# Seven PSUM banks for the first projection, one mixer chunk and one memory weight split earlier, and one sum of squares moved, in a one-core decoder-trunk kernel

## The chip, the cores and the metric

The kernel runs on one core of a Trainium2 chip. The metric is the device time of one execution in microseconds. Three runs of the kernel before took 1888.49, 1888.15 and 1880.31 us; their median is 1888.15.

## What is computed

One layer of a decoder trunk, for a prompt of 1024 tokens and for 8 samples of 4 tokens that look back on 4096 cached positions in pages. The reference, cut to what matters here:

```python
h = rms_norm(x, g_mix)
u, v, cq, ckv, kpe = split_in(h @ w_in)                 # first projection
a_out = gelu(u) * mixed(layer_norm(gelu(v)), w_s, b_s)  # gMLP, chunks of 128
ckv_n = rms_norm(ckv)
q = mla_queries(cq); k, vv = mla_keys_values(ckv_n, kpe)
b_out = attend(q, k, vv)          # prompt: causal; samples: pages of the cache
x = x + concat(rms_norm(a_out), rms_norm(b_out)) @ w_o  # mixer, out projection
mk, mv = mem_kv(rms_norm(mem))                          # 256 memory tokens
x = x + mem_attend(rms_norm(x), mk, mv)
x = x + conv_ffn(rms_norm(x))
```

All matrix products keep single precision by splitting each operand into a high and a low part and adding three products (`mm3`, L185: high with high, low with high, high with low). A split is a rounding cast on ACT (L191, or L195 with a gain) and a subtraction on DVE (L192, L198).

## The kernel before

The 1056 tokens (1024 of the prompt, 32 of the samples) form nine tiles (`TILES`, eight of 128 and one of 32) and three chunks (`CH`: 384, 384, 288). Work follows in stages, each with its own pools of PSUM banks: `phase1` (the first projection), `phase2a` (the prompt's attention), `phase2b` (the samples' attention), `mem_kv`, `mixed`, `out_proj`, `mem_attention`, and the feed-forward part.

*First projection.* `phase1` has a pool `ps1` with five banks "mm" for products and three "st" for small ones. In the loop over two halves (`hf`) it makes v for nine tiles (`proj`, 24 matmuls each), then u for nine tiles, then the gate products. An evicting Gelu on ACT (L435) scales by `rs_tok`, the root of the token's sum of squares, which `squares` (L332 on ACT) and `rsqrt` (a chain of small DVE steps, L222 to L236) make for tiles 0, 1 and 2, 3 to 5 and 6 to 8. `gate_matrices` makes the small constants: `wsc` (POOL, L392) and two products into "st" (L394, L396), which DVE reads at L398.

*Prompt attention.* `phase2a` projects queries (q), keys (k) and values (v) from the latents (`cqh`, `ckh`) for groups of two tiles. A group is a pair of lists of steps: the first makes q and k, the second v. The q and k of groups 0 to 3 run ahead of the transposes; their v runs after the first transposes. From there a table of steps written out by hand sets the order on PE, ACT, DVE and POOL. At its end `mix_steps` normalises the prompt's outputs `b_all`: squares on ACT (L1501), roots on DVE, scaling on ACT (L1506), four transposes on PE (L1511), a copy on DVE (L1512) and a store to `mix_dram`. The roots sit in a ring of two buffers ("mixr"). At the same time `pth`, the transposed probabilities, are copied on ACT (L928) for the value products (L938), and POOL works on sums of down-projection weights (L778 to L781).

*Samples' attention.* `phase2b` runs 128 numbered steps, again in a written order; `at(n, pos, f)` puts a function into step n. In the last steps four raw loads (two of the memory tokens, two of the weights `w_mk`) are issued. Behind it `mem_kv` makes keys and values of the memory: per head a weight is split (`stream`), and the keys are scaled by a product with diagonal matrices ("diag", L1470, L1471). The latents of the last sample are folded (L1380) and copied on ACT (`olT`, L1381), and `end` (L1171) projects them with `wuv`.

*Mixer.* `mixed` loads the normalised rows of `mix_dram` through three raw buffers, two of eight rows at a time, and splits them into `mx0`, `mx1`, `mx2`, one pair per chunk; SP issues its loads in written order: w_o 0, chunk 0, w_o 1, chunk 1, chunk 2. `mixed_sample` adds the samples' part (`n`, L1551 to L1556). `out_proj` multiplies by eight weight tiles and sums squares of the result per chunk in `acc` (POOL, L1603). At its end the three sums over the partitions (L270) and three roots `r3` follow; then `mem_attention` starts with the query products (`query`), 24 matmuls for each head and chunk.

Where no order is written, the recording layer places instructions on each engine by its own ranking.

Of the kernel before, what the change touches and what calls it, by code (L numbers as in the profile page):

```python
# [154 lines left out]
class Net:  # L155
# [132 lines left out]
    def phase1(self):  # L288
        nc, tc, I, O = self.nc, self.tc, self.I, self.O
        p = self.open("p1")  # L290
        pp = self.open("ps1", space=PSUM)
# [87 lines left out]
        def gate_matrices():  # L379
# [13 lines left out]
            st = self.t(pp, [P, 512], F32, "st", 3)  # L393
# [17 lines left out]
        for hf in range(2):  # L411
# [185 lines left out]
    def phase2a(self):  # L597
# [72 lines left out]
        for g in groups[:4]:  # L670
            extra[0] += self.proj_group(p, pp, 0, *g, st[0], c)[1]
# [20 lines left out]
        with tc.manual_schedule(engines={E.PE, E.Activation, E.DVE, E.Pool}):  # L692
# [13 lines left out]
            def mix(G, ring):  # L706
# [3 lines left out]
                yield from self.mix_steps(pm, pp, 1, 2 * G, 2 * G + 2, lambda i: self.b_all[G][:, i % 2], hl, None, ("tp", 4))  # L710
# [345 lines left out]
    def phase2b(self):  # L1056
        nc, tc, I = self.nc, self.tc, self.I
        pa = self.pa3 = self.open("p3a", side="right")
        pt, p = self.open("p3t"), self.open("p3")
# [25 lines left out]
        for n in range(5):  # L1085
            at(2 * n + 2, 0, lambda: next(mix, 0))
        for b in range(NB):
# [22 lines left out]
        def steps(n0, n1):  # L1110
            for n in range(n0, n1):
# [7 lines left out]
                if n > last - 8 and n % 2 == 0 and len(raws) < 4:  # L1119
                    raw = self.t(p, [P, 4, 288], F32, "ck", 15).rearrange("p k n -> p (k n)")[:, : 8 * P]  # L1120
                    src = (I["memT"][:, :4], I["memT"][:, 4:], I["w_mk"][0], I["w_mk"][1])[len(raws)]
# [27 lines left out]
        with tc.manual_schedule(engines={E.SP}):  # L1149
# [5 lines left out]
            mem = self.mem_kv(raws)  # L1155
# [242 lines left out]
    def mem_kv(self, raws):  # L1398
# [10 lines left out]
        mr = [r.rearrange("p (k n) -> p k n", k=4) for r in raws[:2]]  # L1409
# [3 lines left out]
        for h in range(4):  # L1413
            w = self.stream(I["w_mk"][h], 8, raw=raws[2 + h].rearrange("p (k n) -> p k n", k=8) if h < 2 else None)
# [51 lines left out]
        for h in range(4):  # L1466
            bc = self.t(pp, [P, 512], F32, "b", 2)[:, :256]
            for i in range(2):
                dg = self.t(p, [P, P], F32, "diag", 4)
# [20 lines left out]
    def mix_steps(self, p, pp, z, i0, i1, src, hl, nt, tt):  # L1490
# [14 lines left out]
        for i, n in enumerate(ns):  # L1505
            nc.scalar.activation(n, src(i0 + i)[:tn], AF.Copy, scale=r[:, i : i + 1])  # L1506
        yield
        for i, n in enumerate(ns):
# [10 lines left out]
    def mixed(self):  # L1519
# [3 lines left out]
        px = self.open("mx")  # L1523
        pm = self.pm = self.open("pm")
        mxs = [None] * 3
        for c in (0, 2, 1):
            o, n = CH[c]
            if c == 1:
                self.acc = [self.t(pm, [P, 384], F32, f"acc{e}") for e in range(3)]
                self.t(pm, [P, 384], F32, "sqx", 3)  # L1530
            mxs[c] = [self.t(px if c == 0 else pm, [P, 8, n], FR, f"mx{c}{x}") for x in "hl"]
# [28 lines left out]
    def out_proj(self, pp, p, mxs, ws, xh, xl, r3, end):  # L1560
# [45 lines left out]
    def mem_attention(self, xh, xl, r3):  # L1606
        nc, tc, I, O = self.nc, self.tc, self.I, self.O
        pq = self.open("pq")
        pp = self.open("psa", space=PSUM)
        ps_, p = self.open("pas"), self.open("pa")  # L1610
# [105 lines left out]
        def sample_values():  # L1716
# [3 lines left out]
            pT = self.t(ps_, [P, 2, P], F32, "pT")  # L1720
# [16 lines left out]
            sd = self.t(ps_, [P, P], F32, "sd")  # L1737
# [6 lines left out]
        for h in range(4):  # L1744
# [474 lines left out]
def build(tc, I, O, stop=99, tap=None):  # L2219
# [29 lines left out]
    r3 = N.t(xp, [P, 9], F32, "r3")  # L2249
    po = N.open("po")  # L2250
# [45 lines left out]
```

## Time and profile before

| | |
|---|---|
| median of three runs | 1888.15 us |
| profiled execution | 1886.88 us, span 1885.2 us |
| PE, DVE, ACT, POOL busy | 97%, 73%, 49%, 38% |
| mean granted PE clock | 0.986 |

A row by time gives start, duration, engine, line, operation, output and inputs, shape, and in brackets the idle time of the engine just before it and what released it. A row of the windows view gives busy times and the granted clock of a stretch: 1.00 is full speed. The rows of PE that matter stand in the prediction.

### The profile page before, as it was taken

To read this page: it belongs to the slowest core of one execution; us is meant where nothing else is said; L and a number is where in the kernel's file an instruction comes from. 1 tells how busy PE (TensorE), PEld (TensorE's weight loads), DVE (VectorE), ACT (ScalarE), POOL (GpSimd) and SP (SyncE) were. 2 spreads that over 40 slices of the span, in tenths; PEclk is the share of its full clock that TensorE was granted. 3 is DMA by queue.
4 is the path that set the end of the run, shared out by engine and by line. 5 is a ranking of instruction groups with operands and counts; after the bars stand their busy time and mean duration, and the time that the engine had idled before them with its cause. 6 is when DMAs were issued, how large, how long until landed. Compare 5 with 4: busy or idle time off the path is not lost.

```text
span 1885.2 us, 39848 instructions
## 1 busy us (share of the span) xinstructions
PE 1824.5 (97%) x14402; PEld 1756.9 (93%) x14402; DVE 1382.3 (73%) x2883; ACT 929.7 (49%) x1965; POOL 713.4 (38%) x826
## 2 busy tenths in 40 slices
PE   6999899999999999999999999999999999999999
PEld 6999798889999999998799988999999999999999
DVE  6865868666777667877644576788898888888664
ACT  6435676666555555555543355633332333344442
POOL 1221406643545454544213100157777677500000
PEclk9999899999999999999999999999999999999999
DMA  8102203667776566564554335422222222395242
GB/s 289 65 10 69 80 1 130 254 223 194 209 205 179 168 187 171 169 182 145 169 166 134 135 132 164 130 79 70 87 73 93 78 69 80 99 362 164 79 153 76
DMA packets 139783, 260.18 MB, mean 138 GB/s; under 512 B 20545, under 2 KB 82850, under 8 KB 136514
## 3 DMA queue, kind: packets, MB, share of 16 engines
q1 hardware_dynamic: 138722, 256.58, 43.3%
q8 instruction: 114, 1.87, 0.4%
q10 hardware_dynamic: 864, 1.05, 0.2%
q14 instruction: 83, 0.68, 0.1%
HBM read 212.27 MB, written 45.30 MB: 137 GB/s over the span
## 4 chain that ended last, share of the span: by engine, by line
PE 75%; DVE 8%; DMA 5%; issue 5%; ACT 3%; SPq 2%; POOL 1%; DVEq 0%; POOLq 0%; ACTq 0%
PE s L185 13%; PE d L185 12%; PE mm L185 8%; PE b L185 7%; PE F L185 7%; PE X L185 6%; PE E L185 6%; PE A L185 3%; PE y L185 3%; PE o L938 2%; DMA cT<-cT 2%; PE tp L926 1%; SPq L1212 1%; PE tp L185 1%; PE o L1359 1%
## 5 line engine op out<-in xcount | busy, mean ns | idle before, releaser
L185 PE MATMUL s<-w2h,ch 128*128 128x288 f32 (+1 forms) x1024 | 303.7, 297 | 0.0
L185 PE MATMUL s<-w2h,cl 128*128 128x288 f32 (+1 forms) x1024 | 296.0, 289 | 4.7 <-POOL cl L1244 4.7
L185 PE MATMUL s<-w2l,ch 128*128 128x288 f32 (+1 forms) x1024 | 294.6, 288 | 0.0
L185 PEld LDWEIGHTS s<-w2h,ch 128*128 128x128 f32 x1024 | 192.6, 188 | 8.3 <-issue 3.7
L185 PEld LDWEIGHTS s<-w2h,cl 128*128 128x128 f32 x1024 | 192.4, 188 | 6.9 <-POOL cl L1244 6.7
L185 PEld LDWEIGHTS s<-w2l,ch 128*128 128x128 f32 x1024 | 192.8, 188 | 0.0
L1287 DVE TENSOR_REDUCE ss<-sq 128x16 f32<-128x1024 f32 x128 | 155.6, 1215 | 44.6 <-ACT sq L1284 43.9
L1244 POOL TENSOR_TENSOR cl<-cT,ch 128x512 fp32r<-128x512 f32 x64 | 83.3, 1302 | 122.0 <-ACT ch L1240 90.1
L1284 ACT ACTIVATE sq<-s 128x512 f32<-128x512 f32 x128 | 76.6, 598 | 93.8 <-PE s L185 93.8
L1281 ACT ACTIVATE sq<-s 128x512 f32<-128x512 f32 x128 | 76.9, 600 | 78.3 <-PE s L185 78.3
L191 ACT CAST a<-brb 128x528 fp32r<-128x528 f32 x77 | 48.8, 634 | 112.9 <-PE d L185 107.4
L185 PE MATMUL mm<-whi,xh 128*128 128x256 f32 (+3 forms) x288 | 84.3, 294 | 14.8 <-ACT xh L195 10.0
L192 DVE TENSOR_TENSOR a<-brb,a 128x528 fp32r<-128x528 f32 x77 | 54.1, 705 | 58.5 <-ACT a L191 58.4
L185 PE MATMUL d<-a,w 128*128 128x264 f32 x768 | 95.4, 284 | 0.4 <-DVE G L2075 0.4
L185 PEld LDWEIGHTS d<-a,w 128*128 128x128 f32 x768 | 94.3, 188 | 0.6 <-issue 0.6
L185 PE MATMUL mm<-wlo,xh 128*128 128x256 f32 (+3 forms) x288 | 83.8, 294 | 0.0
L185 PE MATMUL mm<-whi,xl 128*128 128x256 f32 (+3 forms) x288 | 83.3, 293 | 0.0
L938 PEld LDWEIGHTS o<-v,pth 128*128 128x128 f32 x576 | 75.7, 197 | 5.1 <-ACT pth L928 3.4
L1946 POOL TENSOR_TENSOR lo<-s,hi 128x1024 fp32r<-128x1024 f32 x20 | 62.9, 3144 | 45.7 <-ACT hi L1945 45.7
L938 PE MATMUL o<-v,pth 128*128 128x64 f32 x576 | 76.1, 274 | 2.1 <-ACT pth L928 2.0
L2001 ACT COPY a<-A 128x264 f32<-128x264 f32 x43 | 16.1, 375 | 118.7 <-PE A L185 113.9
L1240 ACT CAST ch<-cT 128x512 fp32r<-128x512 f32 x128 | 73.5, 628 | 1.3 <-DMA cT<-cT 1.3
(709 smaller groups left out, 6471.1 us busy)
## 6 DMA issues: line engine op xcount, KB each, us to landing
cT<-cT SPq DMA_DIRECT2D x256, 160.0 KB, 2.7
ck<-ck SPq DMA_DIRECT2D x256, 144.0 KB, 3.5
raw<-w_up SPq DMA_DIRECT2D x44, 512.0 KB, 3.6
wsumd<-wsum SPq DMA_DIRECT2D x13, 1024.0 KB, 4.7
actd<-cv SPq DMA_DIRECT2D x44, 264.0 KB, 2.4
brb<-actd SPq DMA_DIRECT2D x44, 264.0 KB, 5.6
wsum<-w_down SPq DMA_DIRECT2D x11, 1024.0 KB, 4.8
raw<-wsumd SPq DMA_DIRECT2D x20, 512.0 KB, 3.7
```

Source lines behind the costliest of these rows:

```text
L185: self.nc.tensor.matmul(out, l, r, start=first and i == 0, stop=last and i == len(seq) - 1)
L191: {"act": nc.scalar.copy, "pool": nc.gpsimd.tensor_copy, "dve": nc.vector.tensor_copy}[eng](hi, src)
L192: low = lambda: nc.vector.tensor_tensor(lo, src, hi, ALU.subtract)
L926: nc.tensor.transpose(tp[:, z * P : z * P + P], u[e][:, jj * P : jj * P + P], self.ident)
L938: nc.tensor.matmul(u["o"][:, e], th[:, z * P : z * P + P], s["v"][:, jj, h % 4], start=j == z == 0, stop=e == 1 and jj == 2 * G + 1)
L1212: dmas.append([nc.sync.dma_start(cT[:, j], I["cT"][bass.ds(rv, 1)].rearrange("a p n -> (a p) n")) for j, rv in enumerate(rvs)])
L1240: nc.scalar.copy(d["h"][:, k], src[k])
L1244: (nc.vector if k else nc.gpsimd).tensor_tensor(d["l"][:, k], src[k], d["h"][:, k], ALU.subtract)
L1281: nc.scalar.activation(sq[:, 0], ps[:, :, n0 : n0 + 256], AF.Square)
L1284: nc.scalar.activation(sq[:, 1], pt.rearrange("p (e d) -> p e d", e=2), AF.Square)
L1287: yield lambda: nc.vector.tensor_reduce(s["ss"][:, g0 : g0 + 2].rearrange("p e (z h) -> p z e h", z=2), sq.rearrange("p z e (h d) -> p z e ...
L1946: eng.tensor_tensor(lo, src, hi, ALU.subtract)
```

## The change

It has five parts. The line numbers of `mix_steps` and of all behind it are higher in the changed kernel by 13 to 20.

1. *First projection.* `phase1` opens a pool `ps0` with seven "mm" banks and one "st" bank. After v of the first half it closes it and opens `ps1` with five and three as before.
2. *Prompt attention.* The v steps of groups 0 and 1 run ahead of the last group's q and k, and those of groups 2 and 3 stay after the transposes.
3. *End of the prompt attention.* The three `mix_steps` that run there scale on POOL with `tensor_scalar` in place of ACT, with one more `yield` before the transposes.
4. *Mixer and memory weight.* `mx0` and the first memory weight `wk0` get buffers that live through `phase2b`. Chunk 0 is loaded in its steps 6 to 12 and split one row at a time; `wk0` is loaded first of the four raw loads, and split two steps before the end. "diag" has three buffers in place of four.
5. *Third sum of squares.* The third `L270` product and its root move into `mem_attention`, behind the first query product; `acc2` lives in an outer pool, and "sx" takes a bank for it. "pT" and "sd" share the ring "pf".

```diff
-        pp = self.open("ps1", space=PSUM)
+        pp, banks = self.open("ps0", space=PSUM), 7
...
-            ps = self.t(pp, [P, 512], F32, "mm", 5)[:tn, :n]
+            ps = self.t(pp, [P, 512], F32, "mm", banks)[:tn, :n]
...
-            st = self.t(pp, [P, 512], F32, "st", 3)
+            st = self.t(pp, [P, 512], F32, "st", 10 - 2 - banks)
...
             if hf == 0:
+                self.close("ps0")
+                pp, banks = self.open("ps1", space=PSUM), 5
                 w = wsplit("v1")
...
-        for g in range(2):
-            for f in gs[g][0]:
-                f()
-        for g in range(2, 4):
-            for f in gs[g][0][:-6]:
+        for fs in (gs[0][0], gs[1][0], gs[2][0][:-6], gs[0][1], gs[1][1], gs[3][0][:-6]):
+            for f in fs:
                 f()
...
-        for g in groups[:4]:
+        for g in groups[2:4]:
             extra[0] += self.proj_group(p, pp, 0, *g, st[0], c)[1]
...
+        self.mx0 = [self.t(px, [P, 8, 384], FR, f"mx0{x}") for x in "hl"]
+        wk0 = [self.t(px, [P, 8, P], FR, f"wk0{x}") for x in "hl"]
...
+        def mixed_load(k):
+
+            raw = place()[:, :768].rearrange("p (k n) -> p k n", k=2)
+            nc.sync.dma_start(raw, self.mix_dram[:, k : k + 2, :384])
+            for e in range(2):
+                at(k + 10 + e, 3, lambda e: self.split(*(x[:, k + e] for x in self.mx0), raw[:, e], self.col("g_ab", k + e)), e)
+
+        for k in range(0, 8, 2):
+            at(k + 6, 0, mixed_load, k)
+        at(last - 2, 3, lambda: self.split(*wk0, raws[0].rearrange("p (k n) -> p k n", k=8)))
...
-            nc.scalar.activation(n, src(i0 + i)[:tn], AF.Copy, scale=r[:, i : i + 1])
+            if tail:
+                nc.gpsimd.tensor_scalar(n, n, r[:, i : i + 1], None, ALU.mult)
+            else:
+                nc.scalar.activation(n, src(i0 + i)[:tn], AF.Copy, scale=r[:, i : i + 1])
         yield
+        if tail:
+            yield
...
-                for k in range(0, 8, 2):
+                for k in range(0, 8 if c else 0, 2):
...
-        for c in range(3):
-            st = self.t(self.ppt, [P, 512], F32, "om"[c % 2], 1)
-            self.tok_sums(st, acc[c], c, self.ones)
-            ct = slice(3 * c, 3 * c + 3)
-            self.rsqrt(p, r3[:, ct], st[:, ct], 1.0 / 1024)
+        for c in range(2):
+            self.token_roots(p, self.t(self.ppt, [P, 512], F32, "om"[c], 1), r3, c)
...
                 query(h, c)
                 if h == 0 and c == 0:
+                    self.token_roots(p, roots, r3, 2)
                     memory()
```

Three places in the order of the built programs. First PE in the first projection, before: `mm_650` is the ninth tile of v, `mm_710` the first of u.

```order
214 L185 MATMUL mm_650<-whi_113,xh_82 32x256
215 L185 MATMUL mm_650<-wlo_114,xh_82 32x256
216 L185 MATMUL mm_650<-whi_113,xl_83 32x256
217 L185 MATMUL mm_710<-whi_223,xh_82 128x256 [waits Activation_49]
218 L185 MATMUL mm_710<-wlo_224,xh_82 128x256 [waits DVE_49]
```

And in the change, where `mm_714` is the first tile of u:

```order
215 L185 MATMUL mm_650<-wlo_114,xh_82 32x256
216 L185 MATMUL mm_650<-whi_113,xl_83 32x256
217 L394 MATMUL st_374<-wsc_372,sel_368 32x32 [waits DMAHW7_49,Pool_49]
218 L396 MATMUL st_374<-cols_58,sel_368 32x8 [waits DMAHW0_49]
219 L185 MATMUL mm_714<-whi_223,xh_82 128x256 [waits Activation_49]
220 L185 MATMUL mm_714<-wlo_224,xh_82 128x256 [waits DVE_49]
```

The constants' product (L394, L396) stood among the tiles of u, behind the first two; now it stands ahead of them all, and waits for POOL. The first matmul of u waits for ACT in both: before, for the Gelu of v's tile 4, now for that of v's tile 7, the last to use that bank under seven.

Second, ACT behind the samples' attention, before: `mx1h` and `mx2h` are high parts of the mixer's chunks, `raw` the loads, `olT` the copy of the last sample's latents, which `end`'s products on PE (L1171) wait for.

```order
1086 L195 ACTIVATE mx1h_15055<-raw_15101,cols_58 128x384 [waits DMAHW7_49]
1087 L195 ACTIVATE mx1h_15055<-raw_15101,cols_58 128x384
1088 L195 ACTIVATE mx1h_15055<-raw_15107,cols_58 128x384 [waits DMAHW0_49]
1089 L195 ACTIVATE mx1h_15055<-raw_15107,cols_58 128x384
1090 L1381 COPY olT_5761<-m_15159 128x16x4 [waits DVE_49,PE_49]
1091 L195 ACTIVATE mx1h_15055<-raw_15113,cols_58 128x384 [waits DMAHW1_49]
1092 L195 ACTIVATE mx1h_15055<-raw_15113,cols_58 128x384
1093 L195 ACTIVATE mx2h_15049<-raw_15119,cols_58 128x288 [waits DMAHW2_49]
```

And in the change (the copy is L1394 there, `end`'s products L1184):

```order
1088 L195 ACTIVATE mx2h_15077<-raw_15128,cols_58 128x288 [waits DMAHW2_49]
1089 L195 ACTIVATE mx2h_15077<-raw_15128,cols_58 128x288
1090 L195 ACTIVATE mx2h_15077<-raw_15134,cols_58 128x256 [waits DMAHW4_49]
1091 L195 ACTIVATE mx2h_15077<-raw_15134,cols_58 128x256
1092 L195 ACTIVATE mx2h_15077<-raw_15140,cols_58 128x256 [waits DMAHW5_49]
1093 L195 ACTIVATE mx2h_15077<-raw_15140,cols_58 128x256
1094 L1394 COPY olT_5772<-m_15163 128x16x4 [waits DVE_49,PE_49]
1095 L191 CAST xh_15150<-res_15190 128x384 [waits DVE_49,Pool_49]
```

The copy moved from between the splits of chunk 1 to behind all of chunk 2's; each pair of splits waits for its load.

Third, PE at the end of the out projection, before: `o` and `m` are banks for the three sums of squares, `b` the first query product.

```order
6413 L270 MATMUL o_16064<-ones_61,acc_2218_15051 128x1 x2
6414 L270 MATMUL m_16083<-ones_61,acc_2219_15052 128x1 [waits PE_49,Pool_49]
6415 L270 MATMUL m_16083<-ones_61,acc_2219_15052 128x1 x2
6416 L270 MATMUL o_16102<-ones_61,acc_2220_15053 128x1 [waits DVE_49,Pool_49]
6417 L270 MATMUL o_16102<-ones_61,acc_2220_15053 128x1 x2
6418 L185 MATMUL b_16159<-xh_15147,hi_16153 128x384 [waits DVE_49,Activation_49]
```

And in the change, first the end of the out projection, then the end of the query's 24 matmuls:

```order
6413 L270 MATMUL o_16068<-ones_61,acc_2222_15079 128x1 x2
6414 L270 MATMUL m_16087<-ones_61,acc_2223_15080 128x1 [waits PE_49,Pool_49]
6415 L270 MATMUL m_16087<-ones_61,acc_2223_15080 128x1 x2
6416 L185 MATMUL b_16145<-xh_15150,hi_16139 128x384 [waits DVE_49,Activation_49]
6417 L185 MATMUL b_16145<-xl_15151,hi_16139 128x384
```

```order
6438 L185 MATMUL b_16145<-xl_15151,hi_16139 128x384 [waits DVE_49]
6439 L185 MATMUL b_16145<-xh_15150,lo_16140 128x384
6440 L270 MATMUL sx_16118<-ones_61,acc_2244_15153 128x1 [waits DVE_49,Pool_49]
6441 L270 MATMUL sx_16118<-ones_61,acc_2244_15153 128x1 x2
6442 L185 MATMUL b_16203<-xh_15150,hi_16139 128x384
```

The third sum (`acc` for chunk 2) moved behind the first query product and into the bank `sx`.

More of the change, by code (lines that the diff above doesn't have):

```diff
@@ L709, in mix @@
                 hl = [x.rearrange("p (k n) -> p k n", k=4) for x in hl]
[L710 removed]
+                yield from self.mix_steps(pm, pp, 1, 2 * G, 2 * G + 2, lambda i: self.b_all[G][:, i % 2], hl, None, ("tp", 4), True)
             mixes, ready = {28: (0, "q"), 29: (2, "q"), 30: (1, "k")}, []
@@ L1521, in mixed @@
         nc, I = self.nc, self.I
-        px = self.open("mx")
         pm = self.pm = self.open("pm")
-        mxs = [None] * 3
-        for c in (0, 2, 1):
+        mxs = [self.mx0, None, None]
+        for c in (2, 1):
             o, n = CH[c]
             if c == 1:
-                self.acc = [self.t(pm, [P, 384], F32, f"acc{e}") for e in range(3)]
+                self.acc = [self.t(pm, [P, 384], F32, f"acc{e}") for e in range(2)]
                 self.t(pm, [P, 384], F32, "sqx", 3)
-            mxs[c] = [self.t(px if c == 0 else pm, [P, 8, n], FR, f"mx{c}{x}") for x in "hl"]
+            mxs[c] = [self.t(pm, [P, 8, n], FR, f"mx{c}{x}") for x in "hl"]
         ws = {}
@@ L1609, in mem_attention @@
         pp = self.open("psa", space=PSUM)
+        roots = self.t(pp, [P, 512], F32, "sx", 1)
         ps_, p = self.open("pas"), self.open("pa")
@@ L2249, in build @@
     r3 = N.t(xp, [P, 9], F32, "r3")
+    N.acc.append(N.t(xp, [P, 384], F32, "acc2"))
     po = N.open("po")
```

27 lines of the change are left out of this document (16 added, 11 removed).

## The prediction

> **What bounds the kernel now.** I read the page first: busy time, then the chain of work that ended last.
>
> ```profile
> PE 1824.5 (97%) x14402; PEld 1756.9 (93%) x14402; DVE 1382.3 (73%) x2883; ACT 929.7 (49%) x1965; POOL 713.4 (38%) x826
> PE 75%; DVE 8%; DMA 5%; issue 5%; ACT 3%; SPq 2%; POOL 1%; DVEq 0%; POOLq 0%; ACTq 0%
> ```
>
> PE is busy 97% of the span and carries 75% of the chain, so a part of this change is worth what it adds to or takes from PE's own time: waits, and stretches where PE runs at half clock. The view by windows shows where these are. Its columns are the window, its length, busy time of PE, PEld, DVE, ACT and POOL, then granted PE clock, DMA share and GB/s.
>
> ```profile
> 60.00:200.00 140.00, 139.92 (x1019) 136.73 (x1018) 92.50 (x320) 61.54 (x166) 35.40 (x51) 1.00 0.14 39
> 200.00:232.00 32.00, 22.83 (x134) 19.87 (x134) 25.50 (x84) 19.79 (x81) 14.05 (x28) 0.87 0.30 99
> ...
> 440.00:889.00 449.00, 445.12 (x3709) 420.69 (x3711) 331.76 (x631) 254.93 (x562) 211.63 (x335) 1.00 0.64 180
> 889.00:965.00 76.00, 66.63 (x434) 57.58 (x427) 48.57 (x117) 40.34 (x83) 17.56 (x24) 0.91 0.60 188
> 957.40:964.20 6.80, 5.21 (x18) 5.14 (x19) 2.76 (x9) 3.52 (x9) 2.00 (x2) 0.50 0.87 266
> 1036.00:1048.00 12.00, 8.74 (x42) 8.61 (x43) 9.95 (x39) 3.82 (x6) 2.71 (x2) 0.72 0.85 300
> ```
>
> From 60 to 200 PE loses 0.1 us at full clock, so a late start there is carried to the end undiminished. The losses stand in the seams that this change touches, at 200, 889 and 1036, where the clock is 0.72 to 0.91, and one more near 424. The samples' attention (440 to 889) loses only 3.9 us.
>
> **The first projection: seven banks, then a new pool.** Rows of PE, ACT, DVE and POOL, from the view by time:
>
> ```profile
> 35.00 0.28 PE L185 MATMUL mm<-wlo,xh 128*128 128x256 f32 x1
> 35.12 0.28 PE L185 MATMUL mm<-whi,xl 128*128 128x256 f32 x1
> 40.23 0.42 PE L185 MATMUL mm<-whi,xh 128*32 128x256 f32 x1 [4.83 <-ACT gv L435]
> ...
> 46.78 1.20 POOL L392 COPY wsc<-ws 128x32 f32<-128x32 f32 x1
> 51.36 0.18 ACT L332 ACTIVATION_READ_ACCUMULATOR a_all<-a_all 32x1 f32 x1
> 52.16 0.15 DVE L222 TENSOR_SCALAR rqx<-ss 128x3 f32<-128x3 f32 x1
> 53.80 0.15 DVE L234 TENSOR_TENSOR rqa<-rqa,rqx 128x3 f32<-128x3 f32 x1
> 53.92 1.64 DVE L446 TENSOR_TENSOR gv<-gv,rv 128x256 f32<-128x256 f32 x3
> 56.20 0.67 DVE L236 SCALAR_TENSOR_TENSOR rs_tok<-rqh,rqy 128x3 f32<-128x3 f32 x1
> 56.90 0.84 ACT L435 ACTIVATE gv<-mm,rs_tok 128x256 f32<-128x256 f32 x2 [1.26 <-DVE rs_tok L236]
> ...
> 45.35 0.41 PE L185 MATMUL mm<-whi,xh 128*128 128x256 f32 x1
> 51.35 0.25 PE L394 MATMUL st<-wsc,sel 128*32 128x32 f32 x2
> 51.96 0.39 PE L185 MATMUL mm<-whi,xh 128*128 128x256 f32 x1
> ...
> 71.97 0.39 PE L185 MATMUL mm<-vgh,wsh 128*128 128x512 f32 x1
> ```
>
> Today the ninth tile of v0 waits 4.83 us for a bank. With seven banks it follows at once and ends at 37.9 (24 matmuls, 0.12 us from start to start). But the next product, u0, now lies in the pool that is opened after the seven banks are closed: as the rows of the change show, the constants' product waits for POOL's wsc (46.78 + 1.20 = 47.98), and u0's first matmul for the Gelu of v0's tile 7, which held its bank. Today it needs only the banks of tiles 4 and 5, whose Gelus follow at once on the one awaited at 40.23, so they are free at about 41. The Gelu of tile 7 needs rs_tok of tiles 6 to 8, and ran in the pair at 56.90 to 57.74.
>
> That pair comes earlier in the change, for two reasons. DVE now finishes rs_tok ahead of the three L446 (1.64 us), which today stand before its last two steps. And the constants' product is done by 48, so that DVE need not wait for it before the chain, which can start when the squares end, at 51.6 instead of 52.16. Its first steps took 52.16 to 53.95; with two more of 0.2, begun 0.6 earlier, rs_tok is there at 53.7, and the Gelus end 0.8 later at 54.5. Bounds: 52.5, if the chain is not interleaved with the other root at all, and 57.7, as today.
>
> Today u0 takes 45.35 to 71.97, which is 26.6 us, and 0.6 of it are the constants' product in its middle and 0.3 the end of a half clock: 25.7 at full clock. In the change PE will have idled from 38, so u0 starts at half clock, and up to 5.2 us of that cost 2.6: it ends at 54.5 + 25.7 + 2.6 = 82.8 instead of 71.97. **+10.8**, bounds 8 and 14. The cover that used to hide the statistics' chain was u0 itself; that is gone.
>
> **The value products of two groups, moved ahead of the wait for ckh.**
>
> ```profile
> 206.31 0.46 PE L185 MATMUL mm<-w2h,ckh 128*128 128x256 f32 x1 [4.61 <-ACT ckh L191]
> ...
> 224.63 0.27 PE L185 MATMUL tp<-wvh,ckl 128*128 128x256 f32 x1
> 224.07 1.71 DVE L856 TENSOR_TENSOR k<-k,hr 128x512 f32<-128x512 f32 x2
> ...
> 229.55 0.42 PE L185 MATMUL s<-kTh,qTh 96*128 96x320 f32 x1 [1.18 <-ACT qTh L195]
> ```
>
> Four tiles of 6 matmuls (24 x 0.12 = 2.9 us) run in the 4.61 us of waiting and are gone from the stretch that ends at 224.7. What is late next is DVE's k, at 225.8; its transposes can then start at 226.2, and the scores at 227.5, not 229.55. **-2**, between -3 and 0.
>
> **The scaling of the prompt's last outputs, from ACT to GpSimd.**
>
> ```profile
> 420.38 1.28 POOL L781 TENSOR_TENSOR wsum<-wsum 128x512 f32<-128x512 f32 x1
> ...
> 423.97 1.33 ACT L1506 ACTIVATE b_all<-b_all,mixr 128x512 f32<-128x512 f32 x2 [2.75 <-DVE rqx L222]
> ...
> 427.09 1.54 PE L938 MATMUL o<-v,pth 128*128 128x64 f32 x6 [0.37 <-ACT pth L928]
> ```
>
> Six 128x512 scalings move. ACT does two in 1.33 us. A GpSimd scaling by a column of that size is not in the trace: from below it is ACT's 0.67, from above the 1.28 of its two-input operation. I take 1.28, the same engine and size. The pair ends at 423.97 + 2.56 = 426.5 instead of 425.3. Behind it on ACT stand the next group's squares (their ring of two is held by it) and behind these pth, which PE waited for at 427.09: late by 1.2 to 1.8. The clears and key squares of the first sample pages then queue behind the last two scalings on GpSimd. **+2**, between -1 (ACT freed of 4 us) and +4. [...]
>
> **The first mixer chunk and one memory weight, split during the samples' attention.**
>
> ```profile
> 891.14 0.38 PE L185 MATMUL b<-ml,hi 128*128 128x256 f32 x1 [1.21 <-DVE ml L198]
> 932.85 0.44 PE L185 MATMUL b<-mx0h,hi 128*128 128x384 f32 x1 [1.01 <-ACT mx0h L195]
> 936.37 0.45 PE L185 MATMUL b<-mx1h,hi 128*128 128x384 f32 x1 [1.27 <-ACT mx1h L195]
> 955.63 0.45 PE L185 MATMUL b<-mx0h,hi 128*128 128x384 f32 x1 [0.77 <-ACT hi L191]
> 958.99 0.63 PE L1556 MATMUL o<-ident,n 32*128 32x32 f32 x4 [2.74 <-ACT n L1553]
> ...
> 932.19 0.61 ACT L195 ACTIVATE mx0h<-raw,cols 128x384 fp32r<-128x384 f32 x1 [4.97 <-DMA o_mk<-kr]
> 948.02 1.71 ACT L195 ACTIVATE mx2h<-raw,cols 128x256 fp32r<-128x256 f32 x4 [1.59 <-DMA raw<-mix]
> ...
> raw<-w_up SPq DMA_DIRECT2D x44, 512.0 KB, 3.6
> ...
> L198 DVE SCALAR_TENSOR_TENSOR mx0l<-raw,cols,mx0h 128x384 fp32r<-128x384 f32 x8 | 4.7, 611 | 1.6 <-ACT mx0h L195 1.6
> ```
>
> Four loads, eight splits on ACT and eight on DVE leave the stretch at 924 to 934, and the later chunks move up. Removed on PE: 1.0 + 1.3 of waiting on mx0 and mx1, 0.8 for the third weight, 2.7 for the samples' n, the 3.4 that the half clock from 957.4 to 964.2 costs, and about 0.8 of the 1.2 at the memory weights, where the split of the first no longer stands ahead of ml: 10. But a wait is added. The copy of the latents (olT) stood behind six mx1 splits on ACT; it now stands behind all eight of mx2. Their loads share three raw buffers with mx1's, and each lands about 3.6 us (the page's median for loads of such a buffer) after one is freed. Counted from today's fourth mx0 load, whose split began at 932.19, the next ones land at 934, 937.5 and 939, and the last splits end at 940. PE has worked off the first 42 matmuls by 937 and waits there, and before that at the latents' fold, behind mx1's splits on DVE: 3.8 given back. **-6**, between -9 and -3.
>
> In the samples' attention the sixteen splits and one weight are 8 x 0.61 + 1.2 = 6.1 us on DVE, which is busy 331.8 of 449 there, with PE waiting 3.9. Mostly hidden: **+1.5**, bounds 0 and 6.1, the latter if DVE were full in just those steps.
>
> **The third sum of squares, behind the first query product.**
>
> ```profile
> 1038.05 0.83 PE L270 MATMUL o<-ones,acc 128*128 128x1 f32 x6 [1.06 <-POOL acc L1603]
> 1041.08 0.66 PE L185 MATMUL b<-xh,hi 128*128 128x384 f32 x1 [2.20 <-DVE r L236]
> ```
>
> Both waits go, 3.3 us, as the query's 24 matmuls (384 wide, so 1.5 times 0.12, or 4.3 us in all) need no roots and cover them: they can start at about 1037, behind the two sums that stay, instead of 1041.08. The half clock that follows until 1046.1 costs another 2 to 3. What is late next is DVE's splits of the memory keys and values, which stand behind the roots. **-5.5**, between -7 and -3.
>
> [...]
>
> Scratch buffers that merely share a ring: 0, since the matmuls that use them already wait for the same tiles.
>
> **Sum.** The profiled execution is 1886.88 us (span 1885.2). 1886.9 + 10.8 - 2 + 2 - 6 + 1.5 - 5.5 = 1887.7. The median of the runs, 1888.15, is 1.3 above the profiled execution, and one run was 1880.31, so I do not correct for it. I predict 1888: no change that a measurement of this kernel can tell, which is about 0.5% or 9.4 us.
>
> **Rivals.**
> 1. *Out projection without waits.* Early mx0 lets the three raw buffers run ahead, mx2's splits end before PE arrives, and the stretch 889 to 965 loses all of its 9.4 us of idle time and the 6.8 of its reduced clock (0.91 of 76): -16, not -6. The sum is 1878. For it: ACT was idle half of that stretch. Against it: olT behind the splits, and loads that take about 4 us.
> 2. *olT waits as long as today's splits.* If mx2's loads come no earlier (the last splits ended at 949.73), PE stands from 937.7 to 950 instead of 940.4: +9.6, and with the clock 1.7 more: 1899. It decides from 940.4 on, each us of landing costing one. For it: the DMA share of 0.60 to 0.87 there.
> 3. *DVE full in the samples' attention.* The splits delay the scores by their whole 6.1 us: 1892.3.
> 4. *The bank change does what its words say.* Tile 8 runs without its wait, and u0 starts at 41: 41 + 25.7 + 2.6 = 69.3 is 2.7 us before today's end, and the sum is 1874.2. Against it: the wait for tile 7's Gelu that stands in the built program.
>
> **How the numbers follow.** Forecast 0.52 (1882 to 1894), first rival 0.13, second 0.20, third 0.10, fourth 0.05. The range is 1877 to 1899, from the first rival to the second. Faster by over 0.5% (below 1878.7) takes most of the first, the fourth and a lower edge of the forecast (every part at its better bound): 0.19. Slower by over 0.5% (above 1897.6) takes most of the second and cases in which the upper bounds of banks, GpSimd and samples meet (+14, +4, +6.1): 0.24. Within: 0.57.
>
> **What would show it.** Right: PE idle from 38 to 54 with a wait on gv L435 ahead of u0, u0's end near 83; no PE wait on acc or r near 1036 + shift, clock 1.0 there; no wait of n; a wait on olT. Wrong: u0 starting before 50, or a PE wait over 5 us at olT, or new waits on cl in the samples' attention. What makes the total wrong first is the bank term, the largest and of one sign.

## The result, and the profile after

| | before | changed |
|---|---|---|
| median of six runs (range) | 1885.36 us (1878.77 to 1888.49) | 1897.46 us (1895.56 to 1899.68) |
| profiled execution, span | 1886.88, 1885.2 us | 1895.56, 1893.9 us |
| mean granted PE clock | 0.986 | 0.984 |

The ratio is 1.007, with an interval of 1.0049 to 1.0091: the change made the kernel slower by 0.7%. The forecast was 1888, "no change", with a chance of 0.57 for less than 0.5% either way. By the ratio the outcome is "slower by over 0.5%", which had 0.24. The time itself lies inside the range that was given, and 0.1 us below the 1897.6 that stood for this outcome, because six runs of the kernel before have a median 2.8 us lower than the three from which the forecast started.

The page of the changed kernel, busy time and the chain of work that ended last:

```profile
PE 1823.2 (96%) x14402; PEld 1756.9 (93%) x14402; DVE 1377.5 (73%) x2883; ACT 924.0 (49%) x1959; POOL 723.7 (38%) x832
PE 76%; DVE 7%; issue 6%; DMA 4%; ACT 2%; SPq 2%; POOL 2%; POOLq 0%; DVEq 0%; ACTq 0%
```

PE does the same 14402 instructions in 1.3 us less busy time, and the span is 8.7 longer: about 10 us of new waiting. Two views say where. First the windows, with the columns of the prediction, for the seams that the change touches:

```profile
450.00:897.00 447.00, 436.58 (x3583) 412.20 (x3585) 322.98 (x615) 251.58 (x557) 211.92 (x333) 0.99 0.65 184
897.00:972.00 75.00, 70.81 (x527) 62.36 (x520) 52.73 (x123) 40.41 (x81) 17.91 (x28) 0.95 0.50 159
1044.00:1056.00 12.00, 12.00 (x89) 12.00 (x87) 9.14 (x31) 6.40 (x11) 5.06 (x5) 1.00 0.41 119
```

The last two rows are the seams at the mixer and behind the out projection, and both are better: the clock went from 0.91 to 0.95 and from 0.72 to 1.00. The row from 450 to 897 is worse: PE loses 10.4 us in the samples' attention, where it lost 3.9. These windows lie 7 to 10 us later than those of the prediction, the work in them 9 to 23 us later, so they don't hold quite the same work.

The second view does: the same PE instruction in both traces, start after minus start before. This is my own subtraction over all PE rows that match in order; the column "step" is the difference from the row above.

| where (start before) | shift | step | forecast |
|---|---|---|---|
| first matmul of the program (9.97) | -0.9 | | |
| first gate product (71.97 to 81.00) | +9.0 | +9.9 | banks +10.8 |
| last key transposes (226.70 to 237.36) | +10.7 | +1.6 | value products -2 |
| a transpose of probabilities (320.97 to 333.95) | +13.0 | +2.3 | none |
| last prompt value products (435.96 to 448.42) | +12.5 | -0.5 | scaling +2 |
| scores of the first samples (455.38 to 474.14) | +18.8 | +6.3 | none |
| out of the samples' attention (925.78 to 948.65) | +22.9 | +4.1 | splits +1.5 |
| mixer's first chunk in the out projection (962.92 to 977.42) | +14.5 | -8.4 | mixer -6 |
| query product (1044.41 to 1053.05), and to the end | +8.6 | -5.9 | third sum -5.5 |

Banks, mixer and third sum are near their forecasts. What the forecast has no step for is 6.3 us at the start of the samples' attention (its +2 for the scaling comes nearest), and 2.3 us at 320; the splits cost 4.1 instead of 1.5, and the value products gained nothing.

### The first projection

Rows by time, of ACT and then of PE:

```profile
52.98 0.84 ACT L435 ACTIVATE gv<-mm,rs_tok 128x256 f32<-128x256 f32 x2 [3.41 <-DVE rs_tok L236]
...
46.80 0.32 PE L394 MATMUL st<-wsc,sel 128*32 128x32 f32 x2 [9.88 <-POOL wsc L392]
53.87 0.58 PE L185 MATMUL mm<-whi,xh 128*128 128x256 f32 x1 [6.68 <-ACT gv L435]
...
81.00 0.40 PE L185 MATMUL mm<-vgh,wsh 128*128 128x512 f32 x1
```

PE does nothing for 9.88 and then 6.68 us. The Gelus that free the bank end at 53.82, forecast 54.5, and the first matmul of u0 follows 0.05 later. The matmuls behind it start 0.21 us apart instead of 0.12, until 57.7, at a granted clock of 0.50: the half clock that was also forecast.

### The start of the samples' attention

The chain of work in the window from 425 to 475 (start, us, what), its pieces that matter here:

```profile
434.79 3.13 POOL b_all L1520 x2
437.94 1.33 ACT k L1514 x4
439.27 0.37 ACT pth L927
439.69 1.12 PE o L937 x6
...
449.62 4.72 DMA mix<-k
454.46 0.34 SPq L1229
...
462.34 2.49 DMA ck<-ck
...
470.41 0.46 POOL krq L1244
470.91 0.79 PE s L1272 x2
```

Two links are new. The scaling on GpSimd leads through the squares on ACT to pth and PE. And the last store of the prompt's outputs, `mix<-k`, must land before SP may issue the first page load of the samples (L1229): 4.72 us, and this link was not in the forecast. From there the chain runs through the page's loads and its statistics to `krq`, for which PE stands 2.37 us at 470.91. At 462.04 it had already stood 2.38 us, there for ACT's S, ahead of an earlier product of the same line. SP's own waits (engine, line, what it waited for: total, times, longest), after and before:

```profile
SPq L1229 <- DMA mix<-k: 4.2, 1, 4.2
```

```profile
SPq L1216 <- DMA mix<-k: 0.5, 1, 0.5
```

No line of the diff touches these loads. The buffers' addresses in the built programs give the connection: `mx0` and `wk0`, which now live through the samples' attention, take 32,768 bytes of each partition, and the first page buffer moves up by so much, from byte 37,536 to 70,304. There it overlaps the tile that the last store of `mix_steps` reads (68,480 to 71,552). Experiment e8 tests this.

### The mixer

Rows by time, of ACT and of PE:

```profile
961.82 0.19 ACT L1394 COPY olT<-m 128x64 f32<-128x64 f32 x1
...
962.06 1.14 PE L1184 MATMUL m<-wuv,olT 128*32 128x64 f32 x17
974.98 0.30 PE L1573 MATMUL o<-ident,n 32*128 32x32 f32 x2 [0.20 <-ACT n L1570]
1051.22 0.42 PE L185 MATMUL b<-xh,hi 128*128 128x384 f32 x1
1055.47 0.28 PE L270 MATMUL sx<-ones,acc 128*128 128x1 f32 x2
```

The waits for mx0 and mx1 are gone, that for n is 0.20 instead of 2.74, and the added wait that was forecast at olT did not come: the copy ended at 962.01, just as PE arrived. In the query product (1051.22) and the third sum behind it (1055.47) PE waits for nothing.

### The profile page after: what moved, and what is told of

It is laid out like the page before. It is cut to its first block, busy times and chain, and to the rows that moved or that the text cites. A ratio compares the mean times of both kernels' runs of the same rounds, so it can differ in the third digit from the quotient of the medians.

```text
span 1893.9 us, 39846 instructions
## 1 busy us (share of the span) xinstructions
PE 1823.2 (96%) x14402; PEld 1756.9 (93%) x14402; DVE 1377.5 (73%) x2883; ACT 924.0 (49%) x1959; POOL 723.7 (38%) x832
## 4 chain that ended last, share of the span: by engine, by line
PE 76%; DVE 7%; issue 6%; DMA 4%; ACT 2%; SPq 2%; POOL 2%; POOLq 0%; DVEq 0%; ACTq 0%
PE s L185 14%; PE d L185 12%; PE b L185 7%; PE mm L185 7%; PE X L185 7%; PE F L185 7%; PE E L185 7%; PE A L185 3%; PE y L185 3%; PE o L937 2%; DMA cT<-cT 1%; PE tp L925 1%; PE o L1372 1%; SPq L1225 1%; POOL cl L1257 1%
```

## The experiments

All but the last four are the changed kernel with one edit. The kernel before ran beside each: its median was 1885.47 in the job of e1, e2, e4 and e5, 1884.2 in that of e6 to e9, and 1884.25 in the last, so a difference between kernels of different jobs is sure to about 1 us. A ratio on record is not that of the two medians and can differ from it by some 0.1%. Prices in us are differences of medians; places are read from the one profiled execution that each kernel has, and the two need not agree to a microsecond or two.

**e1_noA, the old pool from the start.**

```diff
-        pp, banks = self.open("ps0", space=PSUM), 7
+        pp, banks = self.open("ps1", space=PSUM), 5
...
-                self.close("ps0")
-                pp, banks = self.open("ps1", space=PSUM), 5
```

> The changed kernel with the first projection as before: one pool, five banks, opened once. Theory 1 (the trace of the change shows two waits, 9.9 us on wsc and 6.7 us on tile 7's Gelu, and PE behind the products of u 9.0 us later than before): 9 us faster than the changed kernel, and PE idle again for about 4.8 us at the ninth tile. Rival (the products behind it wait for other engines, so that a later start is partly absorbed): 3 to 5 us faster.

1888.81 us, ratio to before 1.0016 (1.0005 to 1.0028): 8.7 less than the changed kernel. At the ninth tile of v the old wait is back, and the two new ones are gone:

```profile
PE mm L185 <- ACT gv L435: 4.2, 1, 4.2
```

The banks cost about 9 us; 10.8 was forecast.

**e4_lateclose, the seven banks kept up to the second half.** If closing the pool is what costs, closing it later should give both: no wait at the ninth tile and none at u0.

```diff
         for hf in range(2):
+            if hf:
+                self.close("ps0")
+                pp, banks = self.open("ps1", space=PSUM), 5
...
             if hf == 0:
-                self.close("ps0")
-                pp, banks = self.open("ps1", space=PSUM), 5
                 w = wsplit("v1")
...
-                ps = self.t(pp, [P, 512], F32, "mm", 5)
+                ps = self.t(pp, [P, 512], F32, "mm", banks)
...
-            st = self.t(pp, [P, 512], F32, "st", 3)
+            st = self.t(pp, [P, 512], F32, "st", 10 - 2 - banks)
```

> The changed kernel with the seven banks kept until the end of the first half, so that u shares their ring and the pool is changed before the second half. Theory 1 (not the seven banks but the change of pools makes the wait): no wait at the ninth tile and none ahead of u, 11 to 14 us faster than the changed kernel, so 2 to 5 faster than with five banks. Rival (with seven banks one bank is left for the small products, and the waits only move to these or to the second half's first tile): 5 to 9 us faster.

1887.28 us, 1.0017 (1.0007 to 1.0026): 10.2 less than the changed kernel, and 1.5 less than e1, between the two expectations. PE no longer waits for a Gelu; what stays is mainly the wait for wsc:

```profile
46.52 0.25 PE L394 MATMUL st<-wsc,sel 128*32 128x32 f32 x2 [2.44 <-POOL wsc L392]
```

So closing the pool in front of u0 cost about 10 us. What seven banks give without that is small: 1.5 us by the medians and 1.3 by the traces (the first gate product starts 3.9 us earlier than in the kernel before, in e1 2.6). The intervals of the two ratios are nearly the same, so this gain is not clear of the noise.

**e5_noB, all value products behind the transposes.**

```diff
-        for fs in (gs[0][0], gs[1][0], gs[2][0][:-6], gs[0][1], gs[1][1], gs[3][0][:-6]):
+        for fs in (gs[0][0], gs[1][0], gs[2][0][:-6], gs[3][0][:-6]):
...
-        for g in groups[2:4]:
+        for g in groups[:4]:
```

> The changed kernel with the value products of all four groups behind the transposes, as before. Theory 1 (the stretch from 210 to 243 lost 1.5 us against before, because the keys' normalisation on DVE, not PE, ends last there): 0 to 2 us faster. Rival (the products fill an idle PE, as predicted): 2 us slower.

1894.46 us, 1.0049 (1.003 to 1.0067): without the move the kernel is 3.0 faster by the medians, though the intervals of the two ratios overlap. PE's longest waits of e5 between 205 and 245, and the row of the first scores behind them:

```profile
PE mm L185 <- ACT ckh L191: 4.6, 1, 4.6
PE s L185 <- ACT qTh L195: 3.6, 2, 2.4
```

```profile
239.46 0.41 PE L185 MATMUL s<-kTh,qTh 96*128 96x320 f32 x1 [1.17 <-ACT qTh L195]
```

And of the changed kernel:

```profile
PE tp L879 <- DVE k L855: 3.4, 2, 3.0
PE tp L879 <- ACT hsq L830: 3.2, 2, 2.8
PE mm L185 <- ACT ckh L191: 1.2, 1, 1.2
PE s L185 <- ACT qTh L195: 0.8, 1, 0.8
```

```profile
239.62 0.63 PE L185 MATMUL s<-kTh,qTh 96*128 96x320 f32 x1
```

The waits are others, but in sum nearly the same, 8.2 and 8.6 us, and the scores start at the same time, although e5 was behind by 1.3 us at 205. The chains on ACT and DVE set the time here, and the value products had been done beside them anyway: filling the wait for ckh with them made new waits for hsq and k. That is a gain of 1.4 us for e5. It gains some 3 us more up to 335, most of it from 328 on, where the changed kernel ran at half clock (last section), and is 3.4 us ahead at 385, but only 0.2 at 975: the two profiled executions, 1895.27 and 1895.56 us, are 0.3 apart. So the 3.0 us of the medians have no single place in the traces.

**e2_noC, the prompt's last scaling on ACT again.**

```diff
-                yield from self.mix_steps(pm, pp, 1, 2 * G, 2 * G + 2, lambda i: self.b_all[G][:, i % 2], hl, None, ("tp", 4), True)
+                yield from self.mix_steps(pm, pp, 1, 2 * G, 2 * G + 2, lambda i: self.b_all[G][:, i % 2], hl, None, ("tp", 4))
```

> The changed kernel with the six scalings of the prompt's outputs back on ACT. Theory 1 (the scalings take 1.55 us each on POOL, the stores of the outputs end later, the first sample pages are loaded behind these, and the samples' attention waits twice for 2.5 us): both waits (on S and krq, near 462 and 471) are gone, and the time is 5 to 8 us below the changed kernel. Rival (the two waits come from the early loads of the mixer chunk, which share the queue with the pages): the waits stay, and the time is within 2 us.

1892.0 us, 1.0041 (1.0028 to 1.0055): 5.5 less. The size is that of the first theory, but the waits are those of the rival: SP still waits for the store, and PE for krq.

```profile
SPq L1229 <- DMA mix<-k: 4.4, 1, 4.4
...
PE s L1272 <- POOL krq L1244: 4.0, 3, 2.1
```

The stores come earlier (the last is issued at 446.55 instead of 449.62), and with them all that hangs on them; the wait for the last one is not the scaling's doing. From this run comes the second theory, that of the addresses.

**e8_kk, the store that collides put elsewhere.** The second of the three `mix_steps` takes its tiles from the ring "k" instead of "q", so that the last two stores lie at bytes 62,336 and 65,408, below the page buffer.

```diff
-            mixes, ready = {28: (0, "q"), 29: (2, "q"), 30: (1, "k")}, []
+            mixes, ready = {28: (0, "q"), 29: (2, "k"), 30: (1, "k")}, []
```

> The changed kernel, with the second of the three row stores moved to the other ring, so that the last one's two tiles lie in other memory than the first page's buffer. Theory 2 (the page's load waits for the memory): SP's wait on the store is gone, the first pages are issued about 4 us earlier behind it, and the time is 3 to 6 us below the changed kernel. Rival (the stores are late because of POOL, and the queue alone holds the pages): no gain, within 1 us.

1892.97 us, 1.0048 (1.0035 to 1.0061): 4.5 less. SP's wait is what it was before the change:

```profile
SPq L1229 <- DMA mix<-k: 0.5, 1, 0.5
```

The product that started at 453.69 before and 17.2 us later in the changed kernel is 13.5 late here. The tile of the fourth of the six stores now lies where the last one's did, and costs SP no wait beyond these 0.5 us. The collision of addresses is shown.

**e7_place, the buffers as in the change, the chunk loaded and split where it was.**

```diff
-        for k in range(0, 8, 2):
-            at(k + 6, 0, mixed_load, k)
...
-                for k in range(0, 8 if c else 0, 2):
+                for k in range(0, 8, 2):
```

> The changed kernel in which the buffers of the first mixer chunk and of the memory weight stay where the change puts them, but the chunk is loaded and split in the mixer stage as before. Theory 2 (the buffers push the first page buffer of the samples' attention onto the memory of the last stored rows, so that the page's load waits for that store to land): the wait of SP on the store (4.2 us) and PE's two waits near 462 and 471 stay; the losses from 485 to 512 go with the early loads, and the gain of 10 us in the mixer stage goes too: 3 to 7 us slower than the changed kernel. Rival (the early loads crowd the queue and the DMA engines): the two waits go.

1901.71 us, 1.0089 (1.0065 to 1.0113): 4.3 more than the changed kernel. SP's wait is there with no early load at all, so it belongs to the buffers:

```profile
SPq L1227 <- DMA mix<-k: 4.4, 1, 4.4
```

Its shift stays near +18 from 455 on, so the loss of 4.1 us is not there, and neither is the mixer's gain. The early chunk alone is thus worth 4.3 us net; the -8.4 in the mixer and +4.1 in the samples' attention of the table above come to the same.

**e6_noE, all three sums ahead of the first query product.**

```diff
-        for c in range(2):
-            self.token_roots(p, self.t(self.ppt, [P, 512], F32, "om"[c], 1), r3, c)
+        for c in range(3):
+            self.token_roots(p, self.t(self.ppt, [P, 512], F32, "om"[c % 2], 1), r3, c)
...
-                    self.token_roots(p, roots, r3, 2)
```

> The changed kernel with all three sums of squares and roots ahead of the first query product, as before. Theory 1 (the two waits come back, with the half clock behind them): 5 to 6 us slower than the changed kernel. Rival (the work behind the query product, on DVE, ends last anyway): within 1.5 us.

1900.21 us, 1.0079 (1.0056 to 1.0102): 2.8 more than the changed kernel, though the intervals of the two overlap. A row of PE by time, and the window of the seam:

```profile
1052.59 0.83 PE L270 MATMUL o<-ones,acc 128*128 128x1 f32 x6 [1.06 <-POOL acc L1622]
```

```profile
1048.00:1060.00 12.00, 10.94 (x66) 10.86 (x65) 11.34 (x40) 5.23 (x10) 3.79 (x3) 0.86 0.68 233
```

The wait of 1.06 for acc is back, and part of the half clock (0.86), but not the 2.20 for the root: so about half of the 5.9 us gained here is the third sum's move (2.8 by the medians, 2.3 by the traces). The rest lies in what e6 keeps, and the built programs of the three kernels say what that is. Before, the first query product lies in PSUM bank 1, the bank of the third sum, which the root reads. In e6 and in the changed kernel "sx" is given a bank ahead of it, and the product lies in bank 2. So the 2.20 us were a wait for a bank, and in e6 PE does not wait for the root, although the root is made ahead of the product as before.

**e9_best: e2, e4, e5 and e8 together.** Early chunk, early weight and moved sum stay.

> The mixer chunk, the weight and the third sum as in the change; seven banks kept until the end of the first half; value products and scaling as before; the row stores as in the run with the other ring. If the parts add up: 10.2 + 5.5 + 3 + 3 to 6 us below the changed kernel's 1897.5, so 1873 to 1876, and about 0.5% faster than before. Rival (the parts share waits, the last two above all): 1877 to 1882.

1874.31 us, 0.994 (0.9922 to 0.9959). The four single gains, 5.5 + 10.2 + 3.0 + 4.5, taken from 1897.46 give 1874.3, so by the medians nothing was counted twice. Part of that is luck. The scaling and the place of the buffers, 5.5 and 4.5 us one at a time, make 5.8 together in the table above. And between 419 and 436 PE in e9 gains 4.1 us on the kernel before, where the code of the two hardly differs: the kernel before ran there at a clock of 0.50 (421.5 to 431.7), e9 at 1.00 (417 to 430). Three windows of it, behind the loads of the chunk:

```profile
470.00:480.00 10.00, 10.00 (x81) 9.94 (x79) 9.66 (x18) 5.98 (x13) 4.43 (x7) 1.00 0.98 265
480.00:490.00 10.00, 6.77 (x51) 6.26 (x50) 9.86 (x15) 4.58 (x10) 4.84 (x5) 1.00 0.82 233
490.00:500.00 10.00, 8.77 (x66) 8.18 (x66) 9.66 (x25) 6.67 (x15) 3.88 (x5) 1.00 0.80 226
```

DVE is busy 9.7 to 9.9 of 10 us in just the steps where the splits stand, and PE loses 4.5 us there.

**e10_spread: e9 with a load every 16 steps instead of every 2.**

```diff
-                at(k + 10 + e, 3, lambda e: ...
+                at(8 * k + 10 + e, 3, lambda e: ...
...
-            at(k + 6, 0, mixed_load, k)
+            at(8 * k + 6, 0, mixed_load, k)
```

> The combined kernel (u on seven banks, value products and scaling as before, stores in the other ring), with the four early loads of the mixer chunk 16 steps apart instead of 2, so that no more than two splits fall into one batch's softmax. Theory 3 (in the combined kernel DVE is busy 9.7 to 9.9 of 10 us in each window from 470 to 500, and PE falls 4.9 us behind there): 3 to 5 us below the combined kernel's 1874.3. Rival (each load takes a page's buffer and crowds the queue): the loss is spread over the four places and the time within 1 us.

1870.82 us, 0.9924 (0.991 to 0.9937): 3.5 less than e9, and the fastest version of all, 0.8% faster than before the change (its clock from 417 to 430 is 1.00 too). The same windows:

```profile
470.00:480.00 10.00, 9.90 (x79) 9.69 (x78) 7.37 (x15) 6.43 (x14) 4.31 (x6) 1.00 0.88 257
480.00:490.00 10.00, 8.16 (x63) 7.75 (x62) 9.47 (x19) 4.59 (x10) 5.26 (x7) 1.00 0.75 197
490.00:500.00 10.00, 10.00 (x70) 10.00 (x69) 8.30 (x21) 5.69 (x12) 4.72 (x8) 0.83 0.76 213
```

DVE has room again in two of the three, and PE stands 1.9 us instead of 4.5. In the third its clock is 0.83, so that the gain in matmuls is smaller: 212 in the three windows instead of 198. The loads are spread with the splits, so which of the two crowded these steps is not separated: the DMA share fell too, from 0.98 to 0.88.

**e11_bestC: e9 with the scaling on GpSimd, as in the change.** The edit is that of e2, reversed.

> The combined kernel with the scaling on POOL, as in the change. Theory 1 (a scaling of 1.55 us on POOL instead of 0.67 on ACT, in the chain that ends with the stores and the first pages): PE waits about 3 us on pth, and the time is 2 to 4 us above the combined kernel's 1874.3. Rival (all that the scaling cost came through the page's memory): within 1 us.

1879.88 us, 0.9977 (0.9966 to 0.9987): 5.6 more than e9, the same price as in e2 without the collision of addresses. PE's waits between 425 and 530:

```profile
PE o L938 <- ACT pth L928: 3.8, 1, 3.8
PE s L1273 <- POOL krq L1245: 2.7, 2, 1.4
```

In e9 PE waits 1.25 us for the same copy, at 423.27, and not at all for krq. The clock has a part in the price: from 417 to 430 it is 0.61 here and 1.00 in e9.

**e12_bestlate: e9 with the chunk loaded and split in the mixer.** The edit is that of e7.

> The combined kernel with the mixer chunk loaded and split in the mixer stage as before, its buffers kept in place. Theory 3 (early loads give 10 us in the mixer stage and take 5 from the samples' attention): 4 to 7 us above 1874.3, with none of the loss between 470 and 500. Rival (the gain in the mixer stage comes from the memory weight and the order of the loads): within 2 us.

1879.76 us, 0.9976 (0.9964 to 0.9989): 5.5 more than e9, and 8.9 more than e10. Not all of this is the chunk's: of the 6.1 us between the profiled executions of e12 and e9, 4.8 lie ahead of the first samples' scores (455.38 in the kernel before), in part from 417 to 430, where e12 has a clock of 0.75 and e9 of 1.00. Behind these scores the early chunk pays 1.2 us, and spread (e10) 6.2.

## Why the prediction was wrong, step by step

The forecast's parts come to +0.8 us, and the traces show +8.7. Four steps failed. The place of the early buffers had no term at all, though it cost 4.5 us by e8. The delay that the scaling hands on was taken for 2 us instead of 5.5 (e2). Together these two make 5.8 us in the table, as they overlap. The value products were counted as a gain of 2 us and cost 1.6. The splits were counted at 1.5 us and cost 4.1. The half clock at 320, 2.3 us, belongs to none of the parts. Against this, mixer, banks and third sum came out 2.4, 0.9 and 0.4 us better than forecast.

**Banks, +10.8: right.** The mechanism (u0 waits for tile 7's Gelu, and the cover of the statistics' chain is gone) is there in the rows at 46.80 and 53.87. By the traces it cost 9.9 us, by e1 8.7, within the bounds of 8 and 14; e4 shows that the closing is the cause.

**Value products, -2: wrong in sign.** The prediction named what is late next, DVE's k, and then still counted 2 us for the matmuls that go. They lay beside the chains of ACT and DVE. Moved, they gained nothing: +1.6 by the trace up to the last key transposes; e5 without the move is 1.4 us better up to the scores, and 3.0 in all by the medians.

**Scaling, +2, "between -1 and +4": wrong in size.** The bound from above wasn't one: a GpSimd scaling by a column took 1.55 us here, not at most the 1.28 of the two-input operation of that size. A row of POOL:

```profile
442.14 3.10 POOL L1520 TENSOR_SCALAR b_all<-b_all,mixr 128x512 f32<-128x512 f32 x2 [1.15 <-DVE mixr L236]
```

A pair takes 3.10 where ACT took 1.33. The route was named rightly (squares, pth, PE), but that PE waits for its whole delay, and the samples' loads for the stores behind it, was not priced: 5.5 us by e2 and 5.6 by e11, of which the clock is a part (0.61 against 1.00).

**Splits in the samples' attention, "mostly hidden: +1.5": wrong in size.** This is the third rival's mechanism, at 4.1 of its 6.1 us; 3.3 of them fall between 511 and 526. The step that failed is the reading of DVE as 331.8 busy of 449: an average over 128 steps said nothing of the eight in which the splits were put. The profile of before would have said it, in a window of 10 us:

```profile
480.00:490.00 10.00, 9.62 (x77) 9.39 (x75) 9.43 (x20) 5.53 (x12) 4.37 (x6) 1.00 0.91 249
```

DVE had 0.57 us left there before anything was added. In the changed kernel the same stretch of work comes some 20 us later. A window and rows by time of DVE, POOL and PE:

```profile
500.00:510.00 10.00, 8.70 (x68) 8.28 (x66) 9.79 (x20) 6.57 (x15) 3.71 (x5) 1.00 0.95 276
...
507.97 1.99 DVE L198 SCALAR_TENSOR_TENSOR mx0l<-ck,cols,mx0h 128x384 fp32r<-128x384 f32 x1
508.00 1.55 POOL L1318 TENSOR_TENSOR S<-S,ss 128x768 f32<-128x768 f32 x1 [3.73 <-DVE ss L236]
511.14 0.40 PE L185 MATMUL s<-w2h,cl 128*128 128x288 f32 x1 [2.12 <-POOL cl L1257]
```

DVE has 0.21 us left. POOL stands 3.73 us for a root that DVE makes late, and PE stands 2.12 for the cl that POOL makes behind that. It is a wait on cl, one of the signs of being wrong that the prediction named; before, the longest of these was 1.6. One split took 1.99 us instead of 0.61, just while POOL worked. So the largest wait hangs on DVE. What the loads added (the DMA share is 0.95) is not separated from it.

**Mixer, -6: right in kind, 2.4 too small.** The clock and most of the waits went as reckoned (not the 0.8 us at the memory weights: PE still waits 1.4 for ml, where it waited 1.21), but the 3.8 us given back at olT did not come, and with them the second rival; the first rival's -16 did not come either. With the shift of 22.9 taken off, the copy ended at 939.1 (forecast 940), and PE was there at 939.1 and not at 937, held up ahead of it by the half clock at 953 (0.50 from 953 to 955). The 1.7 us for the clock in the second rival's sum were an estimate, and no run shows them: in the changed kernel PE did not stop at olT, and the clock was 1.00 from 956 to 972. As the prediction tells them, the 3.8 are waits alone.

**Third sum, -5.5: right in size, half right in kind.** It is 5.9 by the traces. By e6 only about half is the move itself; the wait for the root went because "sx" moved the query product to another bank. The prediction put both waits down to the order, so that the size came out is in part luck. Behind the two waits, of 1.06 and 2.20 us with work between them, the kernel before ran at a clock of 0.50 from 1041 to 1046; in the changed kernel the clock is 1.00 from 1044 to 1056.

**What no step named:** the place of the new buffers, 4.5 us by e8. The prediction gave the early buffers the price of their splits alone, and did not ask what their 32,768 bytes push aside. Without the collision the kernel takes 1893 us, inside the forecast's own 1882 to 1894. The half clock at 320, 2.3 us, was not foreseen either.

So the change has one part that loses by itself (the scaling), one that loses by where a pool closes (the banks), one that moves what was hidden already (the value products), and two that gain, of which one pays for the place that its buffers take.

## What to carry to other kernels

The buffers that are kept longer moved the first page buffer by 32,768 bytes here, onto a tile whose store its load then waited for, 4.2 us: where a buffer's life changes, look, in the built program, which load now waits for which store. Before work is put into "idle" time of an engine, read its busy time in windows as long as the step that it goes into, not over the stage: DVE was busy 9.43 of 10 us in such a window, and 331.8 of 449 in the stage. And before a wait is filled with work from behind it, find what ends last behind it: the value products were hidden there already, and moving them cost 1.6 us in place of a gain. A pool of banks is better closed where its last reader is already done: closed ahead of that, it cost about 10 us here (e4). When versions differ by less than 1%, compare the granted clock stretch by stretch too: 4 us of e9's lead over the kernel before stand at a place that the edits hardly touch.

## What was not expected of the hardware

The same wait was followed by a half clock in one run and by none in another. In the changed kernel and in e5 PE waits 2.08 us for the same product, 0.36 us apart in time; first the changed kernel, a row by time and the window behind it:

```profile
326.90 0.45 PE L185 MATMUL s<-kTh,qTh 96*128 96x384 f32 x1 [2.08 <-DVE pr L910]
```

```profile
328.00:335.00 7.00, 7.00 (x33) 6.92 (x33) 2.21 (x8) 1.86 (x5) 6.60 (x6) 0.54 0.38 156
```

And e5:

```profile
326.54 0.44 PE L185 MATMUL s<-kTh,qTh 96*128 96x384 f32 x1 [2.08 <-DVE pr L910]
```

```profile
328.00:335.00 7.00, 7.00 (x56) 6.77 (x55) 4.25 (x13) 5.26 (x12) 6.36 (x5) 1.00 0.37 152
```

PE did 33 matmuls in these 7 us in the one and 56 in the other, at a granted clock of 0.54 and 1.00. Some 2 us (2.3 in the table) thus came at a place that the change doesn't touch. In the traces of the kernel before and of e8 the same wait of 2.08 us is followed by a clock of 1.00 as well (before: from 317.92 to 324.92), in those of e1, e2, e4, e6 and e7 by one below 1.00. Why was not tried, and as each kernel has one trace, it is open whether the kernel decides it or the execution.
